# Input products of two units at a time (512 columns) in retention and linear attention of a hybrid decoder trunk

## The chip, the cores and the metric

The kernel runs on one core of a Trainium2 chip. The metric is the device time of one execution in microseconds (us); the median of three timed runs stands for a kernel. One more execution was recorded by the profiler.

## What is computed

The reference is a trunk of two layers over 1024 tokens of width 1024, all in 32-bit floats. Cut to what matters:

```
h    = RMSNorm_pre(x) * (1 + scale) + shift          # scale, shift, gate from c @ w_mod
proj = h @ w_in                                      # 1024 -> 3088 columns
aq, ak, av, ag,  rq, rk, rv, rg,  gq, gk, gv, gg, ga = split(proj)
A = sliding_window_attention(rotary(aq), rotary(ak), av) * silu(ag)     # 8 heads, window 128
B = rms_norm(retention(rotary(rq), rotary(rk), rv)) * silu(rg)          # 4 heads, chunks of 128
C = rms_norm(gated_linear_attention(gq, gk, gv, decay(ga))) * silu(gg)  # 4 heads, chunks of 64
x = x + gate * RMSNorm_post(concat(A, B, C) @ w_out)
```

## The kernel before

**Tiles and units.** The tokens are eight tiles of 128 (`t`), taken in four pairs (`p`). The columns of `w_in` are cut into units of 256: `rq`, `rk`, `rv`, `rg` (retention's queries, keys, values, gate), `gqk` (linear attention's queries and keys), `gv`, `gg`, `kv` (attention's keys and values), `aq0`, `aq1`, `ag0`, `ag1`; `o0` to `o3` are the units of `w_out`.

**Products.** A product of a tile with a unit is made in three passes, high with high, low with high and high with low, since each 32-bit number is kept as two rounded parts (`PASSES`). With eight blocks of 128 rows that is 24 matmuls in one PSUM bank (`accum`, called by `project`). The tokens (`h`) are the stationary operand, the weights the moving one, 256 columns wide. `project_T` has weights stationary and two pairs of tiles moving, 512 columns wide.

**Weights.** A unit arrives as four blocks of 256 KB (`st<-in_w_in_dram`) in one of five staging buffers. ACT or DVE rounds a block to its high part (the copy on line 232 or the CAST on line 234), DVE or, for the fourth block, POOL subtracts for the low part (line 608). The units take turns in seven slots of the arena (`PLACE`, `SW`). `load` starts a unit's transfers and conversions; `used` holds TensorE's program back until the unit is meant to be ready.

**Order on TensorE.** Only one program order exists for TensorE, and it is written by hand. The products are the main sequence. Everything else (transposes, scores, state updates, outputs) is a generator called a job. A model clock `clk[0]` advances with each matmul; a job yields a delay from the table `L` (some 130 entries such as `rc1`, `gc2`, a second value for layer 1 under `@1`) or the name of a flag, and `pump` lets it go on when its time has come. `pump` is called after every seven matmuls of 256 columns and after every four of 512 columns, so a job's instructions stand between parts of a product. The other engines get their order from a scheduler that looks at the whole program. PSUM has three banks for products (`mm`) and five for jobs (`aux`).

**Retention.** For each pair of tiles the loop in `layer` goes through `rq`, `rk`, `rv`, and for each through both tiles: six products of 256 columns. Queries and keys go through the rotary turn on DVE (`ret_rot`, lines 1407 to 1412, and the decay factor on line 1793). After the last product of a pair the job `ret_two` starts: it transposes queries and keys (line 266), makes scores, waits for the running state `stR`, and updates it (lines 1842 and 1844).

**Linear attention.** `do_gqk(hf, kk)` makes turned queries or keys for four tiles; `do_gv(p)` makes the values of two tiles and starts `gla_core`; `do_kv(p)` makes attention's keys and values of two tiles and starts `attn_kv`. `gla_core` makes for each of two tiles a batch of scores in four `aux` banks: 12 matmuls of 32 columns for the off-diagonal blocks and 16 of the same size for the diagonal ones, 28 in one go, all with 32 rows of contraction. DVE then copies them out under a mask.

Of the kernel before, what the change touches and what calls it, by code (L numbers as in the profile page):

```python
# [17 lines left out]
P = 128  # L18
D = 1024
S = 1024  # L20
DEPTH = 2
# [29 lines left out]
SW = dict(W00=6, T1=3, W11=4, W10=5, T2=2, T3=0, T4=1)  # L51
TOK = ((1, 2, 3, 4), (3, 4, 0, 1))
PLACE = []
for _t, _w in zip(TOK, (0, 2)):
    _a, _b, _c = (0, 5, 6) if _w == 0 else (6, _w, 5)
    PLACE.append(dict(gg=_w, rg=5, rq=_a, rk=_b, rv=_c, gqk=_a, gv=_b, kv=_c, aq0=_a, aq1=_b, ag0=_c, ag1=_w,
                      o0=_t[0], o1=_t[1], o2=5, o3=6))
# [111 lines left out]
def trunk(ctx: ExitStack, tc: tile.TileContext, ins, cst, out):  # L169
# [103 lines left out]
    def job(gen):  # L273
        jobs.append([clk[0], None, gen])
# [10 lines left out]
    def step(j):  # L285
        try:
# [453 lines left out]
    def project(dst, l, t, w, n=256, ks=range(KT)):  # L740
# [4 lines left out]
        accum(dst, lambda a, k: h[:, a, k, c], lambda b, k: w[:, b, k, 0:n], ks)  # L745

# [966 lines left out]
    def gla_core(l, p, qk, vs):  # L1713

        yield (lat("gc1", l), ("dec", l, p))
        dA, dB, dC, g = dec[(l, p)]
# [26 lines left out]
        for c in range(2):  # L1743
            sp = [aux() for _ in range(4)]
            for s in range(1, 4):
                for h in range(4):
                    r = slice(32 * h, 32 * h + 32)
                    mult(sp[h][:, P + 32 * s:P + 32 * s + 32], kxz[r, s - 1, c],
                         q1[r, P * c + 32 * s:P * c + 32 * s + 32], True, True, 0.054)
            for s in range(4):  # L1750
                for h in range(4):
# [3 lines left out]
                         True, True, 0.054)  # L1755
            for h in range(4):
# [4 lines left out]
        both_ = aux()  # L1761
        for c in range(2):
# [12 lines left out]
            if t < NT - 1:  # L1775
# [7 lines left out]
                flag(("stG", l, t + 1), lat("gc5", l))  # L1783
        job(gla_out(l, (2 * p, 2 * p + 1), both_))
# [11 lines left out]
    def ret_two(l, ts, qkv):  # L1796
# [25 lines left out]
        both_ = aux()  # L1822
        for i, t in enumerate(ts):
# [11 lines left out]
            if t < NT - 1:  # L1835
# [9 lines left out]
                flag(("stR", l, t + 1), lat("rc4", l))  # L1845
        job(ret_out(l, ts, both_))
# [299 lines left out]
    def layer(l):  # L2146
# [41 lines left out]
        for p in range(NP_):  # L2188
            last = p == NP_ - 1
            rr = {}  # L2190
            for name in ("rq", "rk", "rv"):
                w = used(l, name)
                for tt in range(2):
                    t = 2 * p + tt
                    pm = mm()
                    n = 272 if l == 0 and name == "rq" else 256
                    project(pm[:, 0:n], l, t, w, n)
                    src = pm[:, 0:256]
                    if n > 256:
                        job(silu2(pm[:, 256:272], "ssr", srS[t][:, 240:256]))  # L2200
                    if name == "rv":
                        v = t1()
                        copy("rv", v, src)
                        rr[t] = (rr[("rq", tt)], rr[("rk", tt)], v)
                        if tt:
                            job(ret_two(l, (t - 1, t), rr))
                    else:
                        rr[(name, tt)] = ret_rot(t, src, qdec if name == "rq" else kdec)
                    pump()
                if last:  # L2210
                    load(l, {"rq": "gqk", "rk": "gv", "rv": "kv"}[name])
# [20 lines left out]
        def do_gv(p):  # L2232
            for t in (2 * p, 2 * p + 1):
                pm = mm()
                project(pm[:, 0:256], l, t, used(l, "gv"))
                vs[t] = t1()
                copy("gv", vs[t], pm[:, 0:256])
                if t % 2:
                    job(gla_core(l, p, qks[p], (vs[t - 1], vs[t])))
                pump()  # L2240
            if p == NP_ - 1:
                load(l, "aq1")

# [170 lines left out]
```

## Time and profile before

| | |
|---|---|
| median of 3 runs | 966.14 us |
| the three runs | 965.57, 966.14, 972.37 us |
| profiled execution | 976.59 us, of which the span is 974.9 us |
| PE busy | 949.2 us (97%) |
| DVE busy | 672.2 us (69%) |
| ACT busy | 391.8 us (40%) |
| POOL busy | 212.7 us (22%) |
| mean granted TensorE clock | 0.981 |

Engines: PE is TensorE (matmuls), PEld its weight loads, DVE VectorE, ACT ScalarE, POOL GpSimd, SP the engine that issues most DMAs. The profile lists two records for each score matmul and for some other narrow products, so its counts are above those of the program (6957 records against 6021 instructions on PE). In lines of the timeline the columns are start, length (us), engine, source line, operation, output and inputs with shapes, and a count where equal instructions follow each other. In lines of windows they are the stretch, its length, then for PE, PEld, DVE, ACT and POOL the busy us with the number of instructions, then the granted clock, the busy share of the DMA engines and the GB/s. A number behind an engine's row in brackets is idle time before it with what ended it. `arena` is the memory of weights and tokens, `ma` and `mx` hold turned or mixed operands, `smx` and `sm` are small vectors.

### The profile page before, as it was taken

The numbers are of one execution on the slowest core, as the hardware profiler recorded it, in microseconds if no ns is written. First come the engines' busy times: TensorE is split into PE (matmuls) and PEld (weight loads), VectorE is DVE, ScalarE is ACT, GpSimd is POOL, SyncE is SP. The second block draws the span as 40 slices with busy tenths as digits, with TensorE's granted clock in tenths as the row PEclk, the third lists the DMA queues.
The fourth block names the chain that finished last, engine by engine and source line by source line (L and its number), as shares of the span: only waits on it lengthen the run. The fifth ranks groups of instructions, "written<-read, shape, count | busy, mean of one in ns | idle before, by whom it ended". The sixth has DMA issues, their size and how long they took to land.

```text
span 974.9 us, 18925 instructions
## 1 busy us (share of the span) xinstructions
PE 949.2 (97%) x6957; PEld 820.9 (84%) x6957; DVE 672.2 (69%) x1624; ACT 391.8 (40%) x1073; POOL 212.7 (22%) x251
## 2 busy tenths in 40 slices
PE   5999999999999999999999999999999999999996
PEld 2678999899998887778889999998999877777885
DVE  4898756657767778735677597674467578664895
ACT  3367212223323566533455331223233268752441
POOL 1021001222311234421131000122123034450300
PEclk8999999989999999999999999998899999999999
DMA  9944504523334455787456673452213333359983
GB/s 299 326 133 128 153 13 120 163 65 120 111 102 143 137 152 176 223 260 235 172 191 197 214 220 115 124 169 77 59 42 99 119 105 114 109 187 282 313 266 130
DMA packets 139709, 155.02 MB, mean 159 GB/s; under 512 B 15920, under 2 KB 105820, under 8 KB 139616
## 3 DMA queue, kind: packets, MB, share of 16 engines
q1 hardware_dynamic: 134496, 145.30, 47.9%
q10 hardware_dynamic: 5120, 8.51, 2.3%
q8 instruction: 55, 0.90, 0.4%
q14 instruction: 38, 0.31, 0.1%
HBM read 111.30 MB, written 40.37 MB: 156 GB/s over the span
## 4 chain that ended last, share of the span: by engine, by line
PE 86%; DVE 5%; DMA 5%; issue 1%; ACT 1%; POOL 1%; SPq 1%; DVEq 0%; POOLq 0%; ACTq 0%
PE mm L251 62%; PE aux L251 18%; PE aux L266 5%; DMA st<-in_w_mod_dram 1%; DMA aoS<-t 1%; DMA mx<-mixS 1%; DMA xk<-in_x_dram 0%; DMA wm<-in_w_mod_dram 0%; DVE arena L608 0%; POOL sm L756 0%; DVE mx L962 0%; SPq L237 0%; ACT t L232 0%; DMA mixS<-t 0%; DVE acc L442 0%
## 5 line engine op out<-in xcount | busy, mean ns | idle before, releaser
L251 PE MATMUL mm<-arena,arena 128*128 128x256 f32 (+2 forms) x2808 | 471.1, 323 | 2.5 <-ACT arena L966 1.1
L251 PEld LDWEIGHTS mm<-arena,arena 128*128 128x128 f32 x2808 | 401.7, 191 | 44.6 <-issue 2.8
L251 PE MATMUL mm<-arena,mx 128*128 128x512 f32 (+1 forms) x564 | 128.4, 383 | 0.8 <-DMA mx<-mixS 0.8
L251 PEld LDWEIGHTS mm<-arena,mx 128*128 128x128 f32 x564 | 101.6, 188 | 21.9 <-DMA mx<-mixS 1.2
L251 PE MATMUL mm<-arena 128*128 128x512 f32 (+2 forms) x624 | 109.6, 329 | 0.0
L251 PEld LDWEIGHTS mm<-arena 128*128 128x128 f32 x624 | 92.1, 188 | 10.4 <-issue 0.9
L756 POOL TENSOR_TENSOR sm<-sm,mhalf 128x1 f32<-128x1 f32 (+1 forms) x40 | 43.9, 1097 | 213.6 <-DVE sm L755 213.3
L232 ACT ACTIVATE arena<-st 128x512 fp32r<-128x512 f32 x91 | 53.9, 625 | 58.3 <-DMA st<-in_w_in_dram 22.5
L232 ACT ACTIVATE t<-aux 128x512 f32<-128x512 f32 (+1 forms) x86 | 47.7, 591 | 54.9 <-PE aux L266 28.3
L608 POOL TENSOR_TENSOR arena<-st,arena 128x512 fp32r<-128x512 f32 x25 | 36.4, 1457 | 117.3 <-ACT arena L232 67.9
L608 DVE TENSOR_TENSOR arena<-st,arena 128x512 fp32r<-128x512 f32 x71 | 58.5, 849 | 1.4 <-PE mm L251 0.4
L1523 POOL TENSOR_TENSOR smx<-smx,sm 128x512 f32<-128x512 f32 x32 | 35.3, 1102 | 109.5 <-DVE sm L1522 100.6
L442 DVE SCALAR_TENSOR_TENSOR acc<-st,c_act,acc 128x512 f32<-128x512 f32 x60 | 46.3, 772 | 16.8 <-DMA st<-in_w_mod_dram 16.1
L1519 ACT ACTIVATE smx<-smx,sm 128x129 f32<-128x129 f32 x128 | 49.9, 392 | 16.2 <-DVE sm L1516 15.9
L251 PEld LDWEIGHTS aux<-t,mx 32*128 32x128 f32 (+1 forms) x896 | 44.1, 203 | 4.8 <-issue 2.5
L251 PE MATMUL aux<-t,mx 32*128 32x32 f32 (+1 forms) x896 | 45.3, 287 | 0.3 <-DVE t L1583 0.3
L266 PE MATMUL aux<-c_ident,t 128*128 128x128 f32 (+1 forms) x244 | 36.8, 276 | 1.5 <-ACT t L1742 0.8
L232 ACT ACTIVATE t<-mm 128x256 f32<-128x256 f32 x40 | 14.9, 381 | 52.3 <-PE mm L251 52.2
L1577 ACT ACTIVATE t<-aux 128x512 f32<-128x512 f32 x16 | 9.5, 594 | 63.9 <-PE aux L251 55.1
L266 PEld LDWEIGHTS aux<-c_ident,t 128*128 128x128 f32 (+1 forms) x244 | 29.0, 142 | 4.9 <-ACT t L1742 0.9
L1512 DVE COPY_PREDICATED smx<-c_curmask,aux 128x256 f32<-128x256 int32 x64 | 25.1, 446 | 10.3 <-ACT smx L232 6.5
L251 PE MATMUL aux<-t,t 128*128 128x64 f32 (+2 forms) x296 | 29.4, 258 | 0.0
(246 smaller groups left out, 1360.3 us busy)
## 6 DMA issues: line engine op xcount, KB each, us to landing
st<-in_w_in_dram SPq DMA_DIRECT2D x92, 256.0 KB, 3.5
st<-in_w_mod_dram SPq DMA_DIRECT2D x64, 256.0 KB, 2.9
mixS<-t SPq DMA_DIRECT2D x48, 256.0 KB, 2.5
mx<-mixS SPq DMA_DIRECT2D x20, 512.0 KB, 5.5
st<-in_w_out_dram SPq DMA_DIRECT2D x28, 256.0 KB, 3.6
wm<-in_w_mod_dram SPq DMA_DIRECT2D x12, 512.0 KB, 6.9
t<-tabS SPq DMA_DIRECT2D x16, 256.0 KB, 4.1
aoS<-t SPq DMA_DIRECT2D x32, 128.0 KB, 2.9
```

Source lines behind the costliest of these rows:

```text
L232: A.activation(dst, src, AF.Copy)
L251: T.matmul(dst, lhsT, rhs, start=start, stop=stop)
L266: T.transpose(dst, src, idn)
L442: V.scalar_tensor_tensor(acc, wt, c_act[:, k:k + 1], acc, ALU.mult, ALU.add)
L608: e.tensor_tensor(lo, st, f(hi), ALU.subtract)
L756: G.tensor_tensor(r, r, mhalf[:, :w], ALU.pow)
L1512: V.copy_predicated(sv, curmask.unsqueeze(1).to_broadcast((P, 2, P)), pv[:, :, n // P - 1, :])
L1519: A.activation(sm[:, h, :], sm[:, h, :], AF.Exp, bias=mx[:, h:h + 1], accum_out=sums[:, h:h + 1])
L1523: eng("pn").tensor_tensor(sm[:, :, 0:128], sm[:, :, 0:128], rs.unsqueeze(2).to_broadcast((P, 4, P)), ALU.mult)
L1577: A.activation(sq, po, AF.Square)
```

## The change

Four pairs of units are multiplied as one product of 512 columns. A new function `project_2` has the same stationary operand as `project` and moves two weight slots at once; the three passes and eight blocks stay 24 matmuls, half as many as two products of 256 columns.

- **Retention, layer 0:** `rq` alone (272 columns, 16 of them for the decay), then `rk` with `rv`. **Layer 1:** `rk` alone, then `rq` with `rv`. For each pair of tiles there are two lone products and then two of 512. The transfers of `gqk` start after the last lone product; those of `gv` and of `kv` both start after the last product of 512 (before: `gqk` after `rq`, `gv` after `rk`, `kv` after `rv`, each two products apart).
- **Linear attention, both layers:** `do_gv` and `do_kv` become `do_gkv`: `gv` with `kv` as one product of 512 for each tile. `kv`'s products were two in the middle and six at the end; now each stands with its `gv`.
- **Scores:** `gla_core` of a pair waits for that of the pair before; it waits while two jobs have their output banks open (`opened`); while it fills four score banks, no job that has begun may put anything between (`hold`); and it gives TensorE back (`gcs`) after the 12 off-diagonal scores and after 8 of the 16 diagonal ones.
- **Slots and loads:** `PLACE` and `SW` give the units other slots. `aq1` and `ag0` start after the last product of `gv` and `kv`, `ag1` after `aq0`'s use.
- **Delays:** some 60 of the entries of `L` are changed, such as `rc1@1` from 0 to 5.07, `gc2@1` from 0.84 to 2.8, `kv1` from 4.65 to 6.5, `hn1` from 9.25 to 13.42; `gcs` is 0.0 and `gcs@1` 0.1.

The core of the diff:

```diff
+    hold, turn_of, opened = [None], [None], [0]
     def ready(j):
+        if hold[0] is not None and hold[0] is not j and j[3]:
+            return None
...
+    def project_2(pm, l, t, w0, w1):
+        await_flag(("hT", l, t))
+        c = slice((t % 2) * P, (t % 2) * P + P)
+        h = hT[(l, t // 2)]
+        accum(pm.rearrange("p (s n) -> p s n", s=2), lambda a, k: h[:, a, k, c],
+              lambda b, k: both(w0[:, b, k, 0:256], w1[:, b, k, 0:256]))
...
     def gla_core(l, p, qk, vs):
+        if p:
+            yield (0.0, ("core", l, p - 1))
...
         for c in range(2):
+            while opened[0] > 1:
+                yield 0.2
             sp = [aux() for _ in range(4)]
+            hold[0] = turn_of[0]
             for s in range(1, 4):
                 ...                                # 12 off-diagonal scores
+            yield lat("gcs", l)
             for s in range(4):
                 ...                                # 4 of the 16 diagonal scores
+                if s == 1:
+                    yield lat("gcs", l)
+            hold[0] = None
...
-            for name in ("rq", "rk", "rv"):
-                w = used(l, name)
-                for tt in range(2):
-                    ...
-                if last:
-                    load(l, {"rq": "gqk", "rk": "gv", "rv": "kv"}[name])
+            lone, pair = ("rk", ("rq", "rv")) if l else ("rq", ("rk", "rv"))
+            for tt in range(2):
+                ...
+                project(pm[:, 0:n], l, t, used(l, lone), n)
+                rr[(lone, tt)] = ret_rot(t, pm[:, 0:256], decay[lone])
+            if last:
+                load(l, "gqk")
+            for tt in range(2):
+                ...
+                project_2(pm, l, t, *(used(l, n_) for n_ in pair))
+                rr[(pair[0], tt)] = ret_rot(t, pm[:, 0:256], decay[pair[0]])
+                copy("rv", v, pm[:, 256:512])
+                if tt:
+                    job(ret_two(l, (t - 1, t), rr))
+            if last:
+                load(l, "gv")
+                load(l, "kv")
...
-        def do_gv(p):
+        def do_gkv(p):
             for t in (2 * p, 2 * p + 1):
-                project(pm[:, 0:256], l, t, used(l, "gv"))
+                project_2(pm, l, t, used(l, "gv"), used(l, "kv"))
                 copy("gv", vs[t], pm[:, 0:256])
+                job(attn_kv(l, t, pm[:, 256:512]))
...
-        do_gv(2)
-        do_kv(0)
-        do_gv(3)
-        for p in range(1, NP_):
-            do_kv(p)
+        do_gkv(2)
+        do_gkv(3)
+        load(l, "aq1")
         load(l, "ag0")
```

TensorE's program, in layer 1, at the end of retention's last pair of tiles. In the names a number behind `t` or `aux` tells one buffer from another; `mm_7652`, `mm_7705` are the key products of the two tiles, `t_1299_7736` the keys of the last tile after the turn. Before:

```order
L251 MATMUL mm_7652<-arena_73 128x256 x10
L251 MATMUL mm_7705<-arena_73 128x256 x24
L251 MATMUL mm_7744<-arena_151,arena_73 128x256 x7
...
L251 MATMUL aux_7758<-t_1267_7534,t_1253_7441 128x128 x2
L251 MATMUL mm_7744<-arena_151,arena_73 128x256 x17
L251 MATMUL mm_7803<-arena_151,arena_73 128x256 x24
L266 MATMUL aux_7840<-c_ident,t_1273_7575 128x128
...
L266 MATMUL aux_7847<-c_ident,t_1299_7736 128x128
```

After; `mm_7156` is the last product of queries with values, `t_1280_7199` the queries of the last tile after the turn, `mm_7214` the first product of `gqk`:

```order
L250 MATMUL mm_7156<-arena_151,arena_73 128x512 x12
L250 MATMUL aux_7171<-stR,t_1258_7073 128x128
L250 MATMUL aux_7171<-t_1246_6987,t_1266_7112 128x64 x2
...
L250 MATMUL aux_7223<-t_1246_6987,t_1218_6835 128x128 x2
L250 MATMUL mm_7214<-arena_507,arena_73 128x512 x4
L265 MATMUL aux_7248<-c_ident,t_1274_7146 128x128
...
L265 MATMUL aux_7255<-c_ident,t_1280_7199 128x128
```

Before, 48 products of the two value tiles stood between the last key product and the transposes of those keys; now four products of 512 columns stand between the last product that makes queries and the transposes that read them.

VectorE's program at the same place of layer 1. Before, with the turn of the keys (`t_1299_7736`):

```order
L234 CAST arena_73<-st_7769 128x512
L1793 TENSOR_TENSOR t_1293_7694<-t_1293_7694,c_kdec 128x256
L608 TENSOR_TENSOR arena_73<-st_7769,arena_73 128x512
L1407 TENSOR_TENSOR t_1299_7736<-mm_7705,sincos 128x256
L1409 TENSOR_TENSOR tr_7737<-mm_7705,sincos 128x4x32
```

After, with the turn of the queries (`t_1280_7199`); `st_7215` to `st_7279` are staged blocks of `gv` and `kv`:

```order
L233 CAST arena_151<-st_7215 128x512
L233 CAST arena_151<-st_7279 128x512
L1579 TENSOR_TENSOR t_1270_7124<-aux_7115,t_1269_7123 128x512
L1867 TENSOR_TENSOR stR<-stR,aux_7178 64x2x64 x2
L1869 TENSOR_TENSOR stR<-stR,c_cdt 128x256
L613 TENSOR_TENSOR arena_151<-st_7215,arena_151 128x512
L613 TENSOR_TENSOR arena_151<-st_7229,arena_151 128x512
L613 TENSOR_TENSOR arena_151<-st_7242,arena_151 128x512
L1419 TENSOR_TENSOR t_1280_7199<-mm_7156,sincos 128x256
L1421 TENSOR_TENSOR tr_7200<-mm_7156,sincos 128x4x32
```

Ahead of the last turn there stand now two conversions and three subtractions of `gv` and `kv` as well as the state's update; before, one subtraction.

TensorE's program at linear attention's scores in layer 1, first pair; `mx_7210` holds the keys, `t_1337_7487` and `t_1338_7488` the queries, `mm_7569` is a product. Before:

```order
L251 MATMUL aux_8117<-t_1353_8067,mx_7859 128x32
L251 MATMUL aux_8118<-t_1353_8067,mx_7859 128x32
L251 MATMUL aux_8115<-t_1354_8068,mx_7859 128x4x8
L251 MATMUL aux_8116<-t_1354_8068,mx_7859 128x4x8
L251 MATMUL aux_8117<-t_1354_8068,mx_7859 128x4x8
```

After:

```order
L250 MATMUL aux_7581<-t_1337_7487,mx_7210 128x32
L250 MATMUL aux_7582<-t_1337_7487,mx_7210 128x32
L250 MATMUL mm_7569<-arena_151,arena_507 128x512 x4
L250 MATMUL aux_7579<-t_1338_7488,mx_7210 128x4x8
...
L250 MATMUL aux_7582<-t_1338_7488,mx_7210 128x4x8
L250 MATMUL mm_7569<-arena_151,arena_507 128x512 x4
L250 MATMUL aux_7579<-t_1338_7488,mx_7210 128x4x8
```

Four products of 512 columns stand now between the off-diagonal scores (`128x32`) and the diagonal ones (`128x4x8`), and four more within the diagonal ones. In layer 0 (`gcs` is 0.0) all 28 scores stay together.

Over the whole program PE goes from 6021 to 5253 instructions: 1536 matmuls of 256 columns less, 768 of 512 columns more. VectorE, ScalarE, GpSimd and SyncE keep their numbers of instructions and change their order.

More of the change, by code (lines that the diff above doesn't have):

```diff
@@ L54 @@
 for _t, _w in zip(TOK, (0, 2)):
-    _a, _b, _c = (0, 5, 6) if _w == 0 else (6, _w, 5)
-    PLACE.append(dict(gg=_w, rg=5, rq=_a, rk=_b, rv=_c, gqk=_a, gv=_b, kv=_c, aq0=_a, aq1=_b, ag0=_c, ag1=_w,
-                      o0=_t[0], o1=_t[1], o2=5, o3=6))
+    PLACE.append(dict(gg=_w, rg=5, rq=6 if _w else 0, rk=_w if _w else 5, rv=5 if _w else 6, gqk=_w, gv=5, kv=6,
+                      aq0=_w, aq1=5, ag0=6, ag1=_w, o0=_t[0], o1=_t[1], o2=5, o3=6))
 LOG_CLAMP = -24.0
@@ L273, in job @@
     def job(gen):
-        jobs.append([clk[0], None, gen])
+        jobs.append([clk[0], None, gen, 0])
     def flag(name, lat=0.0):
         flags[name] = clk[0] + lat
+    hold, turn_of, opened = [None], [None], [0]
     def ready(j):
+        if hold[0] is not None and hold[0] is not j and j[3]:
+            return None
         need = j[1]
@@ L285, in step @@
     def step(j):
+        turn_of[0] = j
+        j[3] += 1
         try:
@@ L1761, in gla_core @@
         both_ = aux()
+        opened[0] += 1
         for c in range(2):
@@ L1783, in gla_core @@
                 flag(("stG", l, t + 1), lat("gc5", l))
+        opened[0] -= 1
+        flag(("core", l, p))
         job(gla_out(l, (2 * p, 2 * p + 1), both_))
@@ L1822, in ret_two @@
         both_ = aux()
+        opened[0] += 1
         for i, t in enumerate(ts):
@@ L1845, in ret_two @@
                 flag(("stR", l, t + 1), lat("rc4", l))
+        opened[0] -= 1
         job(ret_out(l, ts, both_))
@@ L2240, in do_gv @@
                 pump()
-            if p == NP_ - 1:
-                load(l, "aq1")
-        def do_kv(p):
-            if p == 0:
-                new_kv()
-            for t in (2 * p, 2 * p + 1):
-                pk = mm()
-                project(pk[:, 0:256], l, t, used(l, "kv"))
-                job(attn_kv(l, t, pk))
-                pump()
         do_gqk(0, 0)
         do_gqk(0, 1)
-        do_gv(0)
+        do_gkv(0)
         do_gqk(1, 0)
-        do_gv(1)
+        do_gkv(1)
         do_gqk(1, 1)
-        do_gv(2)
-        do_kv(0)
-        do_gv(3)
-        for p in range(1, NP_):
-            do_kv(p)
+        do_gkv(2)
+        do_gkv(3)
+        load(l, "aq1")
         load(l, "ag0")
@@ L2305, in layer @@
                 if hf:
-                    if l == DEPTH - 1 and g == 0:
+                    if not g:
+                        load(l, "ag1")
+                    elif l == DEPTH - 1:
                         sw_first("W00")
-                    elif l == DEPTH - 1:
-                        load(l, "ag1")
                     else:
-                        load(l, ("ag1", "o2")[g])
+                        load(l, "o2")
         for hf in range(2):
```

34 lines of the change are left out of this document (16 added, 18 removed).

## Prediction

> **What bounds the kernel now.** I read the page first: busy shares, the slices with the clock, the chain that ended last. Then the groups by shape, the waits, and the timeline at the places that the change touches.
>
> ```profile
> PE 949.2 (97%) x6957; PEld 820.9 (84%) x6957; DVE 672.2 (69%) x1624; ACT 391.8 (40%) x1073; POOL 212.7 (22%) x251
> PEclk8999999989999999999999999998899999999999
> PE 86%; DVE 5%; DMA 5%; issue 1%; ACT 1%; POOL 1%; SPq 1%; DVEq 0%; POOLq 0%; ACTq 0%
> ```
>
> TensorE (PE) is busy for 97% of the span and carries 86% of the chain. No other engine is near it. So a saving counts if it shortens TensorE's own stream, and any cost if it makes TensorE stand. The clock row shows two dips below nine tenths after the start. The waits of the stages in question:
>
> ```profile
> PE aux L266 <- ACT t L1742: 0.8, 1, 0.8
> PE aux L251 <- DVE t L1583: 0.3, 1, 0.3
> ACT arena L232 <- DMA st<-in_w_in_dram: 22.5, 9, 6.3
> ```
>
> TensorE waits there 1.1 us in all. The third row is ACT waiting for weights to land, which costs TensorE nothing today.
>
> **The change part by part.** The profiled execution took 976.6 us (span 974.9 and 1.7 around it); the median of the runs is 966.1. I make the sum against 976.6 and then say what it becomes for the median.
>
> *(a) Wider products.* 1536 matmuls of 256 columns go, 768 of 512 come.
>
> ```profile
> 121.80 5.90 PE L251 MATMUL mm<-arena,arena 128*128 128x256 f32 x48
> 127.54 0.38 PE L251 MATMUL aux<-stR,t 128*128 128x128 f32 x2
> ...
> 928.38 5.60 PE L251 MATMUL mm<-arena,ma 128*128 128x512 f32 x24
> 933.82 2.88 PE L251 MATMUL mm<-arena,mx 128*128 128x512 f32 x12
> ...
> 300.30 8.35 PE L251 MATMUL mm<-arena,arena 128*128 128x512 f32 x36
> 308.58 1.65 PE L251 MATMUL aux<-kT,mx 64*128 64x128 f32 x24
> ```
>
> From start to start, 48 narrow products take 127.54 - 121.80 = 5.74 us, 119.6 ns each. 24 wide ones take 5.44 us, 226.7 ns; 36 others 8.28 us, 230.0 ns. A wide one replaces two narrow ones and saves 239.2 - 226.7 = 12.5 ns at best, 9.2 ns by the other row. Times 768: 9.6 or 7.1 us. The narrow regions also hold more short pauses between products and jobs, so I stay near the upper end: **-9** (-7.1 to -9.6). This part is certain in sign: the number of matmuls is fixed.
>
> The Trainium skill, "TensorE: Matmul & The Clock Gate", section "Back-to-back issue gap", gives an isolated gap of N/2.4 + 2.5 ns, that is 109.2 and 215.8 ns here. By that estimate a pair would save only 2.5 ns and the whole 1.9 us. The rows above are longer at both widths and part by more, so they decide.
>
> *(b) Scores in parts, layer 1.* A batch of 28 scores is cut in three by four wide products each time: two more changes between products and scores in each of eight batches, 16 in all.
>
> ```profile
> 234.83 0.38 PE L266 MATMUL aux<-c_ident,mx 128*128 128x128 f32 x2
> 235.14 1.54 PE L251 MATMUL aux<-t,mx 32*128 32x32 f32 x48
> 236.50 0.40 PE L251 MATMUL aux<-t 32*128 32x32 f32 x8
> 236.84 2.27 PE L251 MATMUL mm<-arena,arena 128*128 128x256 f32 x17
> 239.04 1.55 PE L251 MATMUL aux<-t,mx 32*128 32x32 f32 x47
> ```
>
> 28 scores are 56 records. The first 48 take 1.36 us, 28.3 ns each; 56 at that rate would be 1.59 us, and the batch to the next product took 1.70: 0.11 for the change. The 17 products behind it take 2.20 us, where 119.6 ns each gives 2.03: 0.17 more, of which a missing record may explain 0.12. So a change costs 0.11 to 0.31 us; I take 0.22: 16 times that is **+3.5** (1.8 to 5.0). Layer 0 is not cut and pays nothing.
>
> *(c) Half clock.* Two stretches ran at a granted clock of 0.50:
>
> ```profile
> 206.43:209.85 3.42, 3.15 (x61) 2.48 (x60) 2.12 (x6) 1.34 (x6) 0.00 (x0) 1.00 0.03 5
> 209.85:220.09 10.24, 10.24 (x90) 9.95 (x89) 2.70 (x8) 1.06 (x5) 1.34 (x3) 0.50 0.25 77
> 674.05:677.47 3.42, 2.62 (x64) 2.40 (x63) 2.24 (x12) 2.67 (x10) 0.00 (x0) 1.00 0.00 0
> 677.47:691.13 13.66, 13.66 (x103) 12.09 (x102) 2.52 (x9) 2.39 (x8) 1.33 (x3) 0.50 0.23 78
> 281.50:284.90 3.40, 3.40 (x66) 2.93 (x65) 2.53 (x8) 0.65 (x4) 1.11 (x1) 1.00 0.36 101
> ...
> 211.36 2.79 PE L251 MATMUL aux<-t,mx 32*128 32x32 f32 x48
> 213.94 0.63 PE L251 MATMUL aux<-t 32*128 32x32 f32 x8
> 214.50 5.49 PE L251 MATMUL mm<-arena,arena 128*128 128x256 f32 x24
> 219.79 1.15 PE L251 MATMUL aux<-t,mx 128*128 128x64 f32 x8
> ...
> 677.47:691.13 13.66, 8.29 (x29) 6.50 (x27) 0.00 (x0) 0.66 (x2) 0.50 0.23 78
> ```
>
> In the first, the score batch takes 3.14 us instead of 1.70, and 24 narrow products 5.29 us, 220 ns each, 2.4 us too much; seven more before the scores add 0.7 to 1.1. Together about 5.0. In the second the products are busy for 8.29 us (the last row, products alone), of which at most half is loss, 4.1; with 1.4 for the scores about 5. Sum 10 us. The profiled execution lies 10.45 us above the median. I read it so: the undisturbed timed runs have neither stretch. So their removal is worth 10 in the profile and **0 in the median**. Each stretch follows 3.42 us in which TensorE did nearly only small work (61 and 64 matmuls, scores and transposes), once with 3.15 of 3.42 us busy; a like window at 281.50, with products among it, kept its clock. After the change layer 1's scores have wide products between them, which speaks for a full clock.
>
> The same page of the Trainium skill, section "🔬 Part 1: The HAM clock gate (the "warmup" mystery)", halves the clock after an idle window of about 3413 ns. The lengths here, 10.24 and 13.66 us, are three and four of these; but the window before was busy for 3.15 us, so idle time alone does not tell it. By idleness alone the split scores change nothing here, and the sum for the profile would be 10 us higher.
>
> *(d) Waits that go.* The two PE rows of 0.8 and 0.3 us hang on the old delays, which are set longer: **-1.1** (0 if other waits replace them).
>
> *(e) A new wait at the end of retention.* `gv` and `kv` are now converted together, and in VectorE's order two casts, three subtractions and the state's update stand ahead of the last turn, on which TensorE's transposes wait.
>
> ```profile
> 558.05 0.42 DVE L234 CAST arena<-st 128x512 fp32r<-128x512 f32 x1
> 558.58 0.69 DVE L608 TENSOR_TENSOR arena<-st,arena 128x512 fp32r<-128x512 f32 x1
> 554.00 1.70 DVE L608 TENSOR_TENSOR arena<-st,arena 128x512 fp32r<-128x512 f32 x1
> 564.95 0.41 DVE L1407 TENSOR_TENSOR t<-mm,sincos 128x256 f32<-128x256 f32 x1
> ...
> 566.08 0.28 DVE L1680 TENSOR_SCALAR t<-t 128x256 f32<-128x256 f32 x1
> 566.28 0.41 DVE L1793 TENSOR_TENSOR t<-t,c_qdec 128x256 f32<-128x256 f32 x1
> L1567 DVE TENSOR_TENSOR t<-aux,t 128x512 fp32r<-128x512 f32 x16 | 11.0, 688 | 16.3 <-ACT t L232 12.3 <-PE aux L251 3.8
> 194.83 0.57 DVE L1842 TENSOR_TENSOR stR<-stR,aux 64x128 f32<-64x128 f32 x2
> 195.44 0.42 DVE L1844 TENSOR_TENSOR stR<-stR,c_cdt 128x256 f32<-128x256 f32 x1
> 656.87 0.38 PE L251 MATMUL aux<-stR,t 128*128 128x128 f32 x2
> 658.57 4.73 PE L251 MATMUL mm<-arena,arena 128*128 128x512 f32 x23
> ```
>
> VectorE, layer 1: two casts 0.84, a subtraction of the output path (L1567's form) 0.69, the state 0.57 + 0.42, three subtractions 2.07, the turn 1.13 (564.95 to 566.08), the decay 0.41: 6.1 us; with overlap of neighbours rather 5.3, and 3 us more if POOL slows the subtractions to 1.70. The state's update needs TensorE's state step, halfway through the last product, so these stand some 1.8 us before that product's end: done 3.5 to 4.3 us behind it. TensorE has to do meanwhile: the state block 1.70 us (656.87 to 658.57), four wide products 0.91, four transposes of earlier data 0.6: 3.2. A wait of 0.3 to 1.1 us, up to 4 with POOL's slowing. Before, 48 narrow products (5.7 us) lay between. In layer 0, 16 wide products (3.6 us) stand there instead of four, and I expect 0 to 1. I take **+2** for both (0 to 9, the upper end with the slow subtractions in both layers). What is queued behind these transposes on TensorE is the rest of the `gqk` product and all that follows, so the wait counts in full.
>
> The remaining moves (slots, `aq1` and `ag0` starting together, `core` and `opened`) I cost at nothing: their cover is the stretch of 16 and more wide products (3.6 us) ahead of each first use. If that cover fails, the third rival below says what happens.
>
> **Sum.** Profile: 976.6 - 9 + 3.5 - 10 - 1.1 + 2 = 962.0. Median: 966.1 - 9 + 3.5 - 1.1 + 2 = **961.5**.
>
> **The rivals.**
>
> *First: the undisturbed runs of before hold a half-clock stretch too* (the profiler itself costs some us), and the change removes it. For it: the stretches stand at fixed places of the program and follow from its order. Against it: 10.45 and 10 agree well. With one stretch gone 961.5 - 5 = 956.4, with both 951.5. Chance 0.26.
>
> *Second: fewer pauses.* The waits of (e) don't come, since POOL is idle there and casts end early, and the new delays take pauses out of the narrow regions, about 1 us less in each of some five stretches of 25 us. 961.5 - 2 - 5 = 954.5. For it: the pauses between small groups in the narrow regions, as behind the scores in (b). Against: PE is at 97% and cannot give much. Chance 0.14.
>
> *Third, on the slow side: late weights at the end of retention.* `kv`'s blocks are asked for together with `gv`'s: eight blocks in five staging buffers. If VectorE reaches a cast whose block has not landed, the turn behind it waits, and TensorE behind that. For it: ACT's wait row above, up to 6.3 us for one block. Price: 5.5 us in each layer, and standing that long TensorE falls to half clock, 5 us more: 961.5 - 2 + 2 x 10.5 = 980.5. It decides the sign from (975.8 - 959.5) / 2 = 8.2 us for each layer, half clock included. Against it: `gv` and `kv` go into the slots that the last pair product reads, so their conversions start with that product's end, and their first use stands 48 wide `gqk` products later, 48 x 0.227 = 10.9 us, where the landing of eight blocks and their conversion have to fit. Chance 0.13.
>
> *Fourth: half clock comes back* in the changed kernel, in layer 0, where the scores are not cut, or after the wait of (e): 961.5 + 5 = 966.5. Chance 0.08.
>
> *Fifth: the wide product saves little* (2.5 ns a pair, 1.9 us): 961.5 + 7 = 968.5. The rows of (a) speak against it. The Trainium skill's isolated gap, cited above, is its source. Chance 0.03.
>
> **How the numbers follow.** The forecast, 961.5, has 0.36; it reaches from 957 to 966 by the bounds of (a), (b) and (e). About 1% is what a measurement of this kernel can tell from no change: below 956.5 is faster, above 975.8 slower. First and second rival lie below: 0.40. Forecast, fourth and fifth lie between: 0.47. The third lies above: 0.13. The range 949 to 975 holds all but the third and the ends.
>
> **What would show it.** Right: wide products at 227 to 230 ns; scores in groups of 24, 16 and 16 records in layer 1 with gaps of 0.1 to 0.3 us; no stretch at 0.50 near the first scores; a PE wait of some tenths to 2 us for L1419 to L1424 or L1817 at the end of retention. Wrong: wide products at 235 ns or more; a wait on the casts of `gv` and `kv`; the clock at 0.50 in layer 0's scores; or a profile that loses its 10 us while the median loses far more than 5.

## The result and the profile after

The changed kernel takes **978.9 us** (median of 977.9, 978.3, 979.5 and 981.5) where the kernel before took 966.6: a ratio of **1.0119 (1.0074 to 1.0164)**, slower. Forecast were 961.5 us and a range of 949 to 975. The profiled execution took 977.9 us, of which the span is 975.9.

The page of the changed kernel, busy times, clock and chain:

```profile
PE 942.0 (97%) x6189; PEld 772.2 (79%) x6189; DVE 683.2 (70%) x1624; ACT 389.3 (40%) x1073; POOL 212.3 (22%) x251
PEclk9999999999999999999999999999999999998998
PE 79%; DMA 7%; DVE 7%; ACT 2%; issue 2%; SPq 1%; POOL 1%; DVEq 0%; POOLq 0%; ACTq 0%
```

PE's busy time fell by 7.2 us, though the two dips of the clock, worth 10, are gone; and its share of the chain fell from 86% to 79%, DMA and VectorE going from 5% to 7% each. A new dip of the clock stands near the end. Its waits on PE that matter (line, releaser, us in total, times, longest):

```profile
PE mm L250 <- DMA mx<-mixS: 6.3, 2, 5.9
PE aux L265 <- DVE t L1817: 1.5, 2, 0.8
PE mm L250 <- DVE t L1617: 0.9, 1, 0.9
```

The first row is the surprise: before it was 0.8 us in all. Where it stands, in the timeline of the changed kernel, PE, then one line of VectorE (DVE), then SyncE (SP; `SPq` is its queue):

```profile
867.42 11.04 PE L250 MATMUL mm<-arena 128*128 128x512 f32 x48
878.30 2.92 PE L250 MATMUL mm<-arena,mx 128*128 128x512 f32 x12
887.08 2.05 PE L250 MATMUL mm<-arena,mx 128*128 128x512 f32 x4 [5.86 <-DMA mx<-mixS]
889.60 3.33 PE L250 MATMUL mm<-arena,mx 128*128 128x512 f32 x8 [0.47 <-DMA mx<-mixS]
...
879.61 0.69 DVE L2303 SCALAR_TENSOR_TENSOR t<-t,t 128x512 f32<-128x512 f32 x1 [3.20 <-DMA t<-aoS]
...
876.61 0.46 SPq L236 DMA_DIRECT2D t<-aoS  x1
880.33 0.36 SPq L236 DMA_DIRECT2D mixF<-t  x1
880.78 1.00 SPq L236 DMA_DIRECT2D mixS<-t  x2
881.83 0.50 SPq L236 DMA_DIRECT2D mx<-mixS  x1
...
883.19 0.50 SPq L236 DMA_DIRECT2D mx<-mixS  x1
```

The same place before:

```profile
876.12 10.27 PE L251 MATMUL mm<-arena 128*128 128x512 f32 x44
886.23 4.05 PE L251 MATMUL mm<-arena,mx 128*128 128x512 f32 x16
891.08 2.11 PE L251 MATMUL mm<-arena,mx 128*128 128x512 f32 x8 [0.80 <-DMA mx<-mixS]
...
883.05 1.01 SPq L237 DMA_DIRECT2D mixS<-t  x2
884.11 0.50 SPq L237 DMA_DIRECT2D mx<-mixS  x1
885.16 0.36 SPq L237 DMA_DIRECT2D t<-aoS  x1
885.57 0.50 SPq L237 DMA_DIRECT2D mx<-mixS  x1
```

The last output stage multiplies the mixed rows (`mx`, loaded from `mixS`) of one tile after the other. Before, the first half of the second tile's rows was asked for at 884.11, 2.1 us *ahead* of the end of the last gate products (886.23). Now it is asked for at 881.83, 3.5 us *behind* that end (878.30): in SyncE's queue it stands behind the stores of one more gate (880.33 and 880.78), and these wait for that gate's own load of 876.61, on which VectorE stood idle for 3.2 us (the DVE line). TensorE has 12 products to do (2.9 us) and then stands still until 887.08, 5.25 us after the load was asked for. The clock follows (columns as in the windows above):

```profile
882.00:885.40 3.40, 0.00 (x0) 0.00 (x0) 1.41 (x2) 1.07 (x2) 0.00 (x0) 1.00 0.97 218
885.40:892.30 6.90, 4.75 (x10) 3.31 (x11) 1.39 (x3) 0.63 (x1) 0.00 (x0) 0.51 1.01 356
```

After 3.4 us without any matmul the next 6.9 us run at half clock. TensorE has work only from 887.08 on, so this costs about 2.5 us: 12 products take 5.2 us (887.08 to the next start at 892.77, less the 0.47 of waiting) where 12 x 0.227 = 2.7 would do.

To see where the time went, both programs can be cut at the same product (counted in columns of products, which are as many in both). Lengths in us; the column "before" is the kernel before run once more (first experiment), an execution with half clock for 3.4 us each in the first stage and in linear attention of layer 0; the last is the best version found below:

```
stage                              before   changed   changed, ends mended
start, first gates                  119.9     120.7     119.1
retention, layer 0                   63.2      63.6      63.5
linear attention, attention, 0      191.2     188.9     188.9
attention's gates, layer 0           64.0      64.0      65.5
output of layer 0                    97.5      98.8      98.7
gates, layer 1                       24.3      23.7      23.6
retention, layer 1                  104.3     104.9     104.7
linear attention, attention, 1      204.3     208.3     207.4
last outputs, first part             47.7      56.5      46.3
last outputs, the rest               38.0      38.0      38.0
```

The largest row by far is the last output stage, +8.8 us: its waits grew from 0.8 to 7.3 us (5.86, 0.47 and 0.93 for L1956 at 915.7), and half clock adds about 2.5. Then comes layer 1's linear attention with attention, +4.0. Where the wide products are, nothing like a gain of 9 us appears; of the 2.3 that layer 0's linear attention gains, up to 1.7 are the half clock of the column "before".

### The profile page after: what moved, and what is told of

Read it like the earlier page. It is cut to its first block, busy times and chain, and to the rows that moved or that the text cites. A ratio compares the mean times of both kernels' runs of the same rounds, so it can differ in the third digit from the quotient of the medians.

```text
span 975.9 us, 17391 instructions
## 1 busy us (share of the span) xinstructions
PE 942.0 (97%) x6189; PEld 772.2 (79%) x6189; DVE 683.2 (70%) x1624; ACT 389.3 (40%) x1073; POOL 212.3 (22%) x251
## 4 chain that ended last, share of the span: by engine, by line
PE 79%; DMA 7%; DVE 7%; ACT 2%; issue 2%; SPq 1%; POOL 1%; DVEq 0%; POOLq 0%; ACTq 0%
PE mm L250 58%; PE aux L250 16%; PE aux L265 5%; DMA st<-in_w_in_dram 2%; DMA su<-in_w_out_dram 1%; DMA st<-twS 1%; SPq L236 1%; DMA t<-in_x_dram 1%; DMA t<-xs 1%; DMA xk<-in_x_dram 1%; DVE arena L613 0%; POOL sm L768 0%; DMA wm<-in_w_mod_dram 0%; ACT arena L231 0%; ACT smx L1531 0%
## 5 line engine op out<-in xcount | busy, mean ns | idle before, releaser
L250 PE MATMUL mm<-arena,arena 128*128 128x512 f32 (+2 forms) x2088 | 466.5, 374 | 4.7 <-ACT arena L231 1.6
L250 PEld LDWEIGHTS mm<-arena,arena 128*128 128x128 f32 x2088 | 352.3, 188 | 74.2 <-issue 4.9
L250 PEld LDWEIGHTS mm<-arena 128*128 128x128 f32 x576 | 89.4, 188 | 12.5 <-issue 0.9
L231 ACT ACTIVATE arena<-st 128x512 fp32r<-128x512 f32 x91 | 54.8, 628 | 50.3 <-DMA st<-in_w_in_dram 18.3
L231 ACT ACTIVATE t<-aux 128x512 f32<-128x512 f32 (+1 forms) x86 | 48.2, 590 | 61.3 <-PE aux L265 31.4
L613 DVE TENSOR_TENSOR arena<-st,arena 128x512 fp32r<-128x512 f32 x71 | 56.5, 824 | 5.4 <-ACT arena L231 4.3
L250 PEld LDWEIGHTS aux<-t,mx 32*128 32x128 f32 (+1 forms) x896 | 41.1, 186 | 10.9 <-issue 9.7
L231 ACT ACTIVATE t<-mm 128x256 f32<-128x256 f32 x40 | 14.8, 381 | 83.6 <-DVE tr L1422 51.1
L1419 DVE TENSOR_TENSOR t<-mm,sincos 128x256 f32<-128x256 f32 (+1 forms) x48 | 17.9, 374 | 20.6 <-PE mm L250 10.1
L250 PEld LDWEIGHTS aux<-kT,mx 64*128 64x128 f32 x384 | 24.2, 186 | 5.9 <-issue 2.6
```

The source lines that it names most:

```text
L231: A.activation(dst, src, AF.Copy)
L250: T.matmul(dst, lhsT, rhs, start=start, stop=stop)
L613: e.tensor_tensor(lo, st, f(hi), ALU.subtract)
L1419: V.tensor_tensor(d4, s4, cs.unsqueeze(1).unsqueeze(1).to_broadcast((P, nh, 2, 32)), ALU.mult)
```

## The experiments

The kernel before read 966 to 970 us from one place to the next, so ratios to it, taken side by side, are what is compared.

**1. The kernel before, again.**

> The kernel before, unchanged, to read the granted clock of each timed execution. Theory (the prediction's reading): its undisturbed executions take 966 us at a mean clock of 0.99 or more and only an execution of 972 to 977 us shows 0.98, that is, holds the two stretches at half clock. Rival: every execution holds them, the mean clock is 0.98 at 966 us too, and the 10 us between the profiled execution and the median have another cause.

965.1 us, ratio 0.9986 (0.9947 to 1.0026). The line of its profiled execution with span and mean clock:

```profile
core 0: 963.0 us, clock 0.994
```

Its ten executions: 962.8 to 965.4 us at clocks of 0.993 to 0.997 (six), 970.5 and 971.5 at 0.987 and 0.989, 974.1 and 974.9 at 0.984 and 0.981. So the reading of the prediction holds: the number of half-clock stretches differs from one execution to the next of one program, and a difference of 10 to 12 us goes with it. The shortest executions are not quite free of it, though: the profiled one, of 964.8 us, holds 3.4 us at half clock at 283.3 us, worth at most 1.7.

**2. The width alone.** Each wide product becomes two of 256 at the same place; the order on TensorE stays.

```diff
-        accum(pm.rearrange("p (s n) -> p s n", s=2), lambda a, k: h[:, a, k, c],
-              lambda b, k: both(w0[:, b, k, 0:256], w1[:, b, k, 0:256]))
+        for a, b in PASSES:
+            for k in range(KT):
+                for i, w in enumerate((w0, w1)):
+                    mult(pm[:, 256 * i:256 * i + 256], h[:, a, k, c], w[:, b, k, 0:256], ...)
```

> The changed kernel with each product of 512 columns of the new pairs cut in two of 256 at the same place (768 wide become 1536 narrow, same stationary operand, same order of everything else on TensorE). It measures the width alone. Theory: in place, between jobs, the wide products run at 235 to 243 ns and the narrow ones at 121.6 to 124.3, so the width is worth only 3 to 5 us: 978.9 + 3 to 5 = 982 to 984. Rival (the prediction's term a): 9 us, 988. Second rival: nothing, 979.

990.8 us, ratio 1.0226 (1.0173 to 1.0279): 12 more than the changed kernel, more than any of the three. But the stages say where: retention and linear attention of both layers take 7.8 us more, of which 1.7 are half clock and 2.7 longer waits, those for the turn's decay above all; 3.4 are left. Nearly all of the rest, 7.0 us, stands in attention's gates of layer 0, where nothing was edited; that stage's wait for mixed rows makes its length vary from 64.0 to 67.6 us even among runs whose programs are the same up to there (the changed kernel, and experiments 4 and 9). From the starts of neighbouring products in the two traces: in the four stretches a wide one takes 237, 240, 241 and 243 ns, two narrow ones 241, 244, 241 and 248. That is 4.4, 4.7, -0.5 and 4.8 ns for 192 pairs each. In the third stretch one wide product of the changed kernel waits 0.72 us for a weight copy (L231, at 562.0 us), and no narrow one does; without it 4.9 ns are saved there, and **3.6 us** in all. The theory's "3 to 5" fits the stages and rows; the total does not.

Why a wide product costs 237 to 243 ns and not 227, in the changed kernel's timeline:

```profile
144.57 1.17 PE L250 MATMUL mm<-arena,arena 128*128 128x512 f32 x4
145.58 0.60 PE L265 MATMUL aux<-c_ident,t 128*128 128x128 f32 x4
145.94 3.01 PE L250 MATMUL mm<-arena,arena 128*128 128x512 f32 x12
148.78 1.02 PE L250 MATMUL aux<-acc,c_ones 128*128 128x512 f32 x2
...
579.35 3.92 PE L250 MATMUL mm<-arena,arena 128*128 128x512 f32 x16
583.20 1.16 PE L250 MATMUL aux<-t 64*128 64x128 f32 x16
...
921.23 5.60 PE L250 MATMUL mm<-arena,mx 128*128 128x512 f32 x24
926.67 2.88 PE L250 MATMUL mm<-arena,t 128*128 128x512 f32 x12
```

Start to start: four in 1.01 us are 253 ns each, twelve in 2.84 are 237, sixteen in 3.85 are 241; twenty-four with only products around them in 5.44 are 227. It is the first product behind a job that takes longer. Taken one by one in the two traces, 60 wide products that follow a job take 327 ns from start to start and 645 others 230; 59 pairs of narrow ones behind a job take 329 ns and 646 others 235. So a job delays the narrow pair as much (94 ns) as the wide product (96), and the width itself saves about 5 ns a pair.

**3. Layer 1's score batches whole again.**

```diff
-            yield lat("gcs", l)
+            if not l:
+                yield lat("gcs", l)
...
-                if s == 1:
+                if s == 1 and not l:
```

> The changed kernel with layer 1's score batches whole again (28 in one go, as in layer 0). Theory (the prediction's term b): the 16 extra changes cost 3.5 us, and the clock stays full since wide products stand between the batches: 975.4. Rival (term c): a stretch at half clock comes back near the first scores of layer 1 and takes 5 us: 980. Second rival: the changes cost nothing, 979.

981.6 us, ratio 1.0141 (1.0095 to 1.0188). The interval overlaps that of the changed kernel, but the trace shows the rival's half clock. A window before and within the half clock, and the wait that comes with it:

```profile
704.40:707.80 3.40, 2.80 (x61) 2.04 (x59) 3.40 (x17) 1.04 (x4) 0.00 (x0) 1.00 0.02 5
707.80:714.70 6.90, 5.36 (x15) 4.22 (x16) 3.37 (x9) 3.33 (x13) 1.29 (x1) 0.51 0.68 194
...
PE aux L265 <- ACT t L1756: 3.7, 2, 2.0
```

Linear attention and attention of layer 1 take 3.4 us more. With waits taken out, and with half of the time at half clock counted as lost, TensorE's own work there is 4.5 us less (202.17 for 206.63); waits are 3.6 more and half clock costs 4.4. The price of one change is read in the changed kernel's timeline:

```profile
761.64 1.17 PE L250 MATMUL mm<-arena,arena 128*128 128x512 f32 x4
762.74 0.87 PE L250 MATMUL aux<-t,mx 32*128 32x32 f32 x24
763.54 1.20 PE L250 MATMUL mm<-arena,arena 128*128 128x512 f32 x4
764.67 0.65 PE L250 MATMUL aux<-t,mx 32*128 32x32 f32 x16
765.24 1.20 PE L250 MATMUL mm<-arena,arena 128*128 128x512 f32 x4
766.37 0.42 PE L250 MATMUL aux<-t,mx 32*128 32x32 f32 x8
```

Four wide products between scores take 1.13 us (763.54 to 764.67, 765.24 to 766.37), 0.22 more than 4 x 0.227: the cost of one change as forecast, 16 x 0.22 = 3.5 us. The stage, which has the scores' side too, gives 4.5 here and 4.0 between experiments 13 and 15 below. What the cut buys is a full clock near these scores: the changed kernel and eight of the experiments with two cuts (2, 4 to 7, 9, 10, 13) show no half clock there. Experiments 8 and 11, whose jobs stand elsewhere, have it all the same (at 753 to 773 and 746 to 753 us).

**4. The second tile's rows asked for earlier.**

```diff
         m[0] = load_mix(l, 0)
+        m[1] = load_mix(l, 1)
...
-                m[1] = load_mix(l, 1)
                 job(weights())
```

> The changed kernel with the load of the second tile's mixed rows (mixS, for the last output stage) issued directly behind that of the first, ahead of other transfers in SyncE's queue. Theory: the 5.9 us in which TensorE waits for these rows near the end and the half clock behind it (3.4 us) come from the place of that load in the queue: the wait falls below 2 us, no half clock at 885 us, 978.9 - 4 - 3.4 = 971.5. Rival: the rows themselves are late (the gate's chain), or the weights' transfers slow the load wherever it stands: the wait stays above 4 us and the time at 977 to 979.

975.8 us, ratio 1.0072 (1.0040 to 1.0104): 3 us less by the medians, but the interval overlaps that of the changed kernel, so the gain is not settled. The wait for the second tile is gone, and the next load is late instead:

```profile
883.88 5.68 PE L250 MATMUL mm<-arena,mx 128*128 128x512 f32 x24
...
909.58 1.17 PE L250 MATMUL mm<-arena,ma 128*128 128x512 f32 x4 [3.70 <-DMA ma<-mixS]
```

**5. Seven delays of the end at their old values, with the earlier load** (`sw1`, `ld2`, `ld2@1`, `swW10`, `swW11`, `lay1@1`, `ag1@1`).

> The changed kernel with the last output stage's transfers as they were: seven delays at their old values (sw1 1.3, ld2 0.8, ld2@1 3.08, swW10 1.3, swW11 0, lay1@1 1.5, ag1@1 6.85), so that five of the summed weights' transfers (twS) come later in SyncE's queue, and the load of the second tile's mixed rows directly behind the first's. Theory: the 8.8 us that the stage of the last outputs takes more than before (5.9 us of waiting for mixS, 3.4 us of half clock behind it) come from the order in SyncE's queue: 978.9 - 7 to 9 = 970 to 972, no wait over 1.5 us for mixS after 850 us. Rival: the gates are late whatever stands in the queue: the wait moves to the next load (as with the earlier load alone, where 3.7 us of waiting for the next pair's rows came up) and the time stays at 975 to 979.

978.5 us, ratio 1.0102 (1.0070 to 1.0134). A miss: the last stage's first part is 5.1 us shorter in the profiled execution (51.4), but 3.2 us of waiting stay there: the old values put also the first tile's load later (4.7 us behind the start of the 48 last gate products, where it was 1.9 ahead). The total did not follow: `ld2` acts in layer 0 too, and attention's gates of layer 0 take 3.8 us more in this execution (2.2 of waiting for mixed rows, the rest mostly half clock).

**6 and 7. One pairing undone at a time**, the delays left new: `do_gv` and `do_kv` as before (6), retention's loop over `rq`, `rk`, `rv` as before (7).

```diff
-        do_gkv(0)
+        do_gv(0)
...
-            lone, pair = ("rk", ("rq", "rv")) if l else ("rq", ("rk", "rv"))
+            for name in ("rq", "rk", "rv"):
```

> The changed kernel with linear attention's values and attention's keys and values apart again, as 256-column products in the old order (384 wide products become 768 narrow); retention stays paired, the delays stay new. Theory: this pairing is worth what narrow and wide rows between jobs differ by, 3.5 us in clean rows, 1 to 2 in interrupted ones: 980 to 982.5. Rival: it costs more in the attention stage of layer 1 than it saves (linear attention and attention of layer 1 take 4 us more than before without half clock): undone, 976 to 978.

> The changed kernel with retention's six products of 256 columns for each pair of tiles again, in the order queries, keys, values; linear attention stays paired, the delays stay new, and the transfers of gqk, gv and kv start after the last product. Theory: retention's pairing saves nothing, since the narrower stream's 3.5 us are spent on longer wide products between jobs (237 to 241 ns) and on the wait for the last turn (1.5 us): 977.5 to 980.5. Rival (the prediction's term a): it saves 3.5 to 4.8, undone 982.5 to 984.

991.5 us, ratio 1.0236 (1.0179 to 1.0294), and 988.8, ratio 1.0196 (1.0147 to 1.0244). Both theories and both rivals miss, on the high side. In the stages that were edited (6) costs 7.4 us and (7) 7.8; without waits and half clock 3.6 and 2.5 are left. The rest of the total arises elsewhere. These totals do not price a pairing: each of the two edits, under a table of delays set for other code, costs 10 to 13 us, most of it in waits.

**8. All old delays under the new code.**

> The changed kernel with every delay of the table that existed before at its old value (only the two for the cut of the scores are kept). Theory: the new delays set the order in which jobs reach SyncE and TensorE in layer 1's attention and at the end, and about 9 to 13 of the lost us come with them: 966 to 970. Rival: the old delays fit the old durations of products; with the new code they put jobs ahead of their data, TensorE waits, and the time is 982 or more.

1059.2 us, ratio 1.0911 (1.0852 to 1.0970): the rival, and far beyond it. All 67 delays that differ went back. The mean clock is 0.942, and TensorE waits for the turn's decay and for the mixed rows:

```profile
PE aux L265 <- DVE t L1817: 14.1, 4, 4.7
PE mm L250 <- DMA mx<-mixS: 9.7, 1, 9.7
```

So the new delays are not what made the kernel slower as a whole; without them the pairs cost 80 us more.

**9. The changed kernel again**, beside the next three.

> The changed kernel again, unchanged, beside the next three in the same place, since the kernel before reads 966 to 970 us from one place to the next. Theory: 1.2% above the kernel before, 979 to 982, and each execution shows the half clock behind the wait for mixS near the end (mean clock at or below 0.992).

978.2 us, ratio 1.0112 (1.0059 to 1.0164); clocks 0.986 to 0.993.

**10. The earlier load, and the weights' transfers later** (`sw1` at 1.3 instead of 0.61, beside the edit of 4).

> The changed kernel with two edits at the end: the second tile's mixed rows are loaded directly behind the first's (as before in an experiment), and the summed weights' transfers are issued at the old pace (sw1 1.3 instead of 0.61), five of them later. Theory: the first edit took the wait for the second tile away but the next rows (ma) came late behind the weights' transfers; with both, no wait over 1.5 us for mixS after 850 us, no half clock there, 7 to 9 us less than the changed kernel. Rival: the wait moves on to a third place (mixF or the summed weights themselves), and no more than 4 us are won.

**970.2 us**, ratio 1.0008 (0.9983 to 1.0034): 8.0 us less than the changed kernel beside it. PE at the end:

```profile
871.09 11.04 PE L250 MATMUL mm<-arena 128*128 128x512 f32 x48
881.97 5.66 PE L250 MATMUL mm<-arena,mx 128*128 128x512 f32 x24
887.46 5.60 PE L250 MATMUL aux<-arena,mx 128*128 128x512 f32 x24
```

No wait, and no half clock there. The theory holds in its amount: the first part of the last outputs takes 46.3 us where experiment 9 has 54.0 and the kernel before 47.7, so the 8.8 us there are the order in SyncE's queue. Two edits do it together, and the earlier load is in neither kernel; `sw1` alone was not run.

**11. Old delays of layer 1's attention.**

> The changed kernel with the delays of attention in layer 1 at their old values (aq1, aq2, aq3, aq4, aq5, aq6, aq7, kv1 for layer 1, and pf3, pf4). Theory: the attention stage of layer 1 takes 9 us more than before while linear attention ahead of it takes 5 less; the sum of 4 us is mostly the cut of the scores (3 us) and longer wide products, not these delays, so the time stays within 3 us of the changed kernel or rises. Rival: these delays bunch attention's jobs; old ones give the 4 us back.

985.4 us, ratio 1.0182 (1.0137 to 1.0227): as the theory had it, these delays do not give the 4 us back. The stage takes 214.0 us for 208.3, 3.4 of that half clock; and the waiting for mixed rows grows to 14.6 us, 10.5 of it once near the end, so these delays too reach the last stage.

**12. The kernel before with layer 1's scores cut.**

> The kernel before with layer 1's score batches cut in three as in the changed kernel (four matmuls of 512 or seven of 256 columns between; the pairs are left alone, delays old). Theory: 16 changes at 0.2 us cost 3.5 us against executions without half clock (966 + 3.5 = 969.5), and no execution shows half clock near 677 us; its clock is then steadier than before's. Rival: the cut costs nothing (966), or moves jobs so that other waits come (975 and more).

1000.5 us, ratio 1.0325 (1.0293 to 1.0356). The second rival: other waits come, as this one for ScalarE's copy of the same batch, and the half clock does not go: it stands at 730 to 751 us, 771 to 778 and, behind a wait of 4.9 us for mixed rows, 908 to 915.

```profile
PE aux L251 <- ACT t L1750: 4.8, 2, 4.6
```

**13. Experiment 10 with `fin1` at its old 5.21.**

> The changed kernel with the two edits at the end (earlier load, later weights), and the delay fin1 at its old value 5.21 instead of 4.27, which lets the first gates' evictions of layer 1 go ahead of three subtractions on VectorE. Theory: the 1.4 us that TensorE waits there for L1617 falls below 0.5, and 1 to 2 us are won against 970.2: 968 to 969.5, within 1% of the kernel before and perhaps under it. Rival: the wait moves to the next eviction, 970 to 971.

**966.8 us**, ratio **0.9977 (0.9952 to 1.0001)**: 3.4 less than experiment 10 by the medians, more than expected; but the two ran in different places and their intervals overlap. The wait at the layer's boundary:

```profile
PE mm L250 <- DVE t L1617: 0.7, 1, 0.7
```

In experiment 10 it was 1.4, and 0.8 more stood ahead of it for L1896, which is gone. It did not fall below 0.5 as the theory had it. This is the best version of the study; against the kernel before it is no difference that can be told.

**14 and 15. The same with one cut of the scores, and with none.**

> As the run with fin1 at its old value, but layer 1's score batches are cut once only (12 and 16). Theory: a change costs 0.2 us, eight fewer give 1.6 us, and with four wide products of work in the middle the clock stays full: 966.5 to 968. Rival: half clock comes back in layer 1's linear attention as with whole batches, 970 to 974.

> As the run with fin1 at its old value, but layer 1's score batches are whole. Theory: whole batches save 3.2 us of changes and bring back half clock (5 us) and 2 to 3 us of waiting for ScalarE's copies: 971 to 974. Rival: with the end mended only the saving is left: 965 to 967, below the kernel before.

978.8 us, ratio 1.0094 (1.0057 to 1.0132), and 971.5, ratio 1.0034 (1.0008 to 1.0060). Half clock came back with either, in layer 1's linear attention (at 706 to 709 and 733 to 736 us, and at 708 to 712 and 736 to 739). 15 fell within its theory's 971 to 974; 14 went the way of its rival and beyond it, since it moves other jobs too (4.6 us of waits in attention for the copies of L1434 and L1435, and 2.2 for mixed rows near the end). Two cuts are worth about 5 us against none: they cost 4.0 us of TensorE's own work (206.4 for 202.4 in the stage) and save 4.5 of waits, above all those for ScalarE's copies (L1756), and 3.4 of half clock.

## Why the prediction was wrong, step by step

Between the profiled executions the stages add up to +13.0 us where the sum had -4.6, a miss of 17.6. The first part of the last outputs makes 8.8 of it. The four stages of retention and linear attention, which the sum had priced, make 7.3 (they took +2.7: 0.4 - 2.3 + 0.6 + 4.0). The other stages make 1.5.

- **"The remaining moves ... I cost at nothing": this is the step that failed most.** The sum has no term for the delays of the end, nor for the order of loads in SyncE's queue. The reason given was a cover of "16 and more wide products (3.6 us) ahead of each first use". Ahead of the second tile's first use in the last outputs stood 12 products (2.9 us), and the rows came 5.25 us after a load that was itself 3.5 us late. The price was 8.8 us by the stages: 6.5 more waiting and about 2.5 of half clock. By the medians of experiments 9 and 10, 8.0 us come back. No rival named that place; the third rival had the right mechanism (late transfers, TensorE standing, half clock behind it, sign to the slow side), but at the end of retention, where no product waited for the weights of `gv` and `kv`. Which of the delays made the load late stays open.
- **(a) Wider products, -9: right in sign, too large; this term was mis-sized.** Between jobs the width is worth 3.4 us by the stages and 3.6 by the rows (experiment 2). The narrow row of 119.6 ns holds a product behind a job: from start to start its first takes 204 ns and the other 47 take 117.7, so two narrow ones take 235 and not 239.2. The wide ones take 230 between jobs and not 226.7. So 5 ns are left of 12.5, and the fifth rival (1.9 us) came nearer than -9. The remark that narrow regions hold more pauses is not borne out: a job delays either width by about 95 ns.
- **(b) Scores in parts, +3.5: right**, 0.22 us a change on the products' side and 4.0 to 4.5 in the stage, within its 1.8 to 5.0. That the cut keeps the clock full in layer 1 was right for the changed kernel too (experiments 3, 14 and 15).
- **(c) Half clock: read rightly** in the main (experiment 1); worth next to nothing in the median, as said. But a new stretch came behind the new wait, about 2.5 us.
- **(d) Waits that go, -1.1:** they went, but in layer 1's linear attention and attention two others took their place, 0.6 us for L1803 and 1.1 for L231, so the term came to nothing, as its bound of 0 allowed.
- **(e) The last turn behind the conversions, +2: right in amount, in part by luck.** Of the 1.5 us in two waits for L1817, 0.8 stand at the end of layer 0's retention (180.9 us), where 0 to 1 was expected. At the end of layer 1's, where the working put most, no wait came: the eight transposes of 642.29 us follow the product ahead of them without idle time. The other 0.7 stand behind layer 1's first pair of tiles (578.9 us), where no conversion of `gv` or `kv` is near.
- **Layer 1's linear attention and attention, +4.0,** is the price of the cut, term (b), with hardly a saving from the width against it. With waits and half clock taken out the stage takes 206.6 us for 202.8 before; with whole batches 202.2 and 202.4 (experiments 3 and 15). Its waits are 1.6 us before and 1.7 after.
- **Bounds.** By the bounds of (a), (b) and (e) as they stand the forecast reaches from 957.2 to 971.9, not to 966; and 961.5 - 5 is 956.5. Measured were 978.9, above either.

Experiment 13 does not show the forecast's gain of 4.6 us either. Its median lies 2.7 us under that of the kernel beside it, but the interval includes no change, and the kernel beside it holds more half clock (median clock 0.990 for 0.996). The profiled execution of 13 spans 964.1 us with no half clock ahead of the last products, that of experiment 1 spans 963.0 with two stretches of 3.4 us. So the forecast failed on what it did not count and, by nearly as much, on what it counted.

## What to carry to other kernels

Price a wider matmul from the starts of neighbouring products in the place where it will stand, and keep the first product behind a job apart: in a row of 48 a single one made 119.6 ns out of 117.7. When a table of delays sets an order, a change has to be followed to every queue that the table feeds, down to the last stage: ask of each load there whether it is still issued ahead of the end of the work that covers it. And if only one edit is undone under delays set for the whole, the total shows the disorder, not the edit; compare stages cut at the same work.

## What was not expected of the hardware

Half clock comes without any idle time on TensorE by the profile: in experiment 1 after 3.40 us that were busy throughout, mostly with scores, column sums and transposes. The same stretch of the program, with as many matmuls, kept its clock in the profiled execution of the kernel before that stands ahead of the change. Experiment 1, then that one:

```profile
279.90:283.30 3.40, 3.40 (x72) 3.10 (x70) 1.07 (x6) 0.68 (x4) 0.00 (x0) 1.00 0.44 106
283.30:286.70 3.40, 3.40 (x10) 2.73 (x9) 1.89 (x5) 0.77 (x2) 0.00 (x0) 0.50 0.45 119
...
286.46:289.86 3.40, 3.40 (x72) 3.10 (x70) 1.07 (x6) 0.68 (x4) 0.00 (x0) 1.00 0.46 109
289.86:293.00 3.14, 3.14 (x16) 2.60 (x15) 2.66 (x7) 0.77 (x2) 0.00 (x0) 1.00 0.42 113
```

The 12 products behind that stretch took 4.42 us in the one (from 283.27) and 2.85 us in the other (from 289.83). So it differs from one execution to the next at the same place: the same program ran from 962.8 us at a mean clock of 0.996 to 974.9 at 0.981. Half clock also comes after 3.40 us with no matmul at all (the changed kernel, 882.00 to 885.40). The Trainium skill, "TensorE: Matmul & The Clock Gate", section "🔬 Part 1: The HAM clock gate (the "warmup" mystery)", speaks of an idle window of about 3.4 us; the second case agrees with it, the first (3.40 of 3.40 us busy) does not by idle time alone.
